# State-space heads of a two-block model: one full-height product spreads a head's step rows, two heads' half-width products alternate, and the scheduler's matmul costs are changed

## The chip, the cores and the metric

The kernel runs on one core of a Trainium2 chip. The metric is the device time of one execution in microseconds (us). Engines are named as the profile names them: PE is the matrix engine (TensorE), PEld its weight loads, DVE the vector engine, ACT the scalar engine, POOL the general engine (GpSimd), SP the engine that issues the transfers.

## What is computed

The program is a model of two blocks for 512 tokens of width 1024. Block 1 is a hybrid mixer, cross attention over a memory and a gated feed-forward part; block 2 has a layer with a long convolution (layer A) and a layer with sparse attention (layer B). The change is in the mixer's state-space part (SSD), 16 heads of 64 columns in two groups of 8, tokens in 4 chunks of 128:

```python
adt = (dt * a)...                       # a step per token and head
a_cs = jnp.cumsum(adt, axis=-1)         # cumulated within a chunk
seg = jnp.exp(where(causal, a_cs[l] - a_cs[s], -inf))
cb = einsum("bclgn,bcsgn->bgcls", cc, bc)
y_diag = einsum("bghcls,bcsghp->bclghp", cb * seg, xc)
y_off = einsum("bclgn,cbghpn,bghcl->bclghp", cc, prev, exp(a_cs))
y = y_diag + y_off                      # then + d_skip * xs, times silu(z)
```

`prev` holds the states at the starts of the chunks.

## The kernel before

All activations lie with the channels on the partitions and the 512 tokens along the row. Dense products run in three float32r products each (`mm3`): the weight and the activation are both split into a high and a low part (`whi`/`wlo`, and pairs of `act` tiles). Weights come by SP in tiles `raw`; ACT copies the high part `whi`, DVE subtracts to get the low part `wlo`. The dense results go to the PSUM banks `mm` (3 of them); the SSD part uses the banks `A` (2), `B` (2) and `C` (1).

Instructions are not issued in program order. Class `Program` records them all (each matmul, copy and transfer with an estimated duration `o.dur` and its dependencies, `rec`), then orders each engine's queue by a list schedule (`order`): priorities come from a pass over the reversed program (`latest`) blended with the last forward pass, 12 times over, and the best of the orders by its own estimate is emitted (`emit`). So every engine's queue is one fixed list, worked off strictly in that order, and the estimates decide where everything stands. All instructions are emitted at one line, which is why the profile calls nearly all of them L378.

The SSD part for one head:
- `head_a(hh)`: PE spreads the head's row of cumulated steps over all 128 partitions into a bank `A`. The weight is one column of `sel`, repeated; the moving operand is `arow`, rows of heads, split in a high and a low tile of 16 partitions, so that there are two products. DVE subtracts the head's column `acs` (a constant whose name in the profile is `dt`), takes min with 0, ACT the exponential, DVE multiplies by `cb`. The result is the tile `m`. ACT and POOL make `ce`, the decayed C rows, from the same bank.
- `head_b(hh)`: seven products, four with `m` and three with `ce`, each with a weight of 128 x 64 and a moving operand of 128 x 128 in float32, go to one half (64 partitions) of a bank `B`. Two heads share a bank. After the second, DVE adds the skip term from the bank and multiplies by `z`.
- `states(g, c)`: four transposes to a bank `C`, two DVE products from it, one product of 128 x 512 in float32 into a bank `B`, and the running state.

A loop over 18 steps calls `head_a(hh)`, and `head_b` two heads behind. Around it stand, in the program, the pool branch (`v_tile`, `p_tile`, and `om_pool`, whose 8 tiles of the output projection do not need the heads), and behind it the keys and values of the memory (`k_proj`, `v_proj`) and the output projection of the SSD branch.

In layer A, `conv_tile(j)` makes one of 12 channel tiles: one product with a diagonal matrix from `pad` into a bank `B`, then 19 multiply-adds by DVE on that bank (`B<-pad,vec,B` in the profile), the taps.

Of the kernel before, what the change touches and what calls it, by code (L numbers as in the profile page):

```python
# [17 lines left out]
P = 128  # L18
T = 512
# [39 lines left out]
class View:  # L59
    """a lazily resolved access pattern of a tile"""  # L60
# [61 lines left out]
class Program:  # L122
    """records instructions in program order, then orders each engine's by a list schedule"""
# [13 lines left out]
    def rec(s, eng, fn, m, args, kw):  # L137
# [27 lines left out]
        if eng == "PE":  # L165
            one = m == "transpose" or args[1].base.dt == F32R
            o.table = n > 8
            o.dur = n / 2.4 * 2 if m == "transpose" else max(107, n / 2.4) + 2.5 if one else max(27, n / 2.4) * 4
# [27 lines left out]
    def latest(s, prio):  # L196
        """latest starts, from a list schedule of the reversed program"""
# [35 lines left out]
    def order(s, prio, window):  # L233
# [9 lines left out]
        # slots in use if the rest ran in program order: a tile may take one early only if this never exceeds the number there is  # L243
# [137 lines left out]
def body(ctx, tc, t, out):  # L381
# [25 lines left out]
    def bank(tag):  # L407
        return new(pp, (P, T), F32, tag, True)
# [114 lines left out]
    class LN:  # L523
        """layer norm over tiles that come one by one, centred first by the mean of the first npil tiles, whose sum is then 0"""
# [29 lines left out]
        def finish(s):  # L554
            """broadcast rows r, q with norm = centred * r - q"""
# [36 lines left out]
    # ================= block 1, mixer =================  # L592
# [27 lines left out]
    # time steps of all heads  # L620
# [30 lines left out]
    # softplus(x) = max(x, 0) + log1p(exp(-|x|)), log1p(e) = 2 atanh(e / (2 + e))  # L651
# [20 lines left out]
    # cumulated steps as rows of heads  # L672
    ps = bank("B")[0:16, :]
    for c in range(4):
        TE.matmul(ps[:, c * P:(c + 1) * P], adt[:, c * 16:(c + 1) * 16], triu, start=True, stop=True)
    arow = split(ps)
    sel = const("sel", (16, 16), F32R)
    S.activation(sel, ident[0:16, 0:16], AF.Copy)
# [10 lines left out]
    # causal convolution of xs, B, C; order of the channel tiles: B0 B1 C0 C1, then xs  # L689
# [15 lines left out]
    # z gate  # L705
# [7 lines left out]
    # B in token rows, B C products  # L713
# [48 lines left out]
    def head_a(hh):  # L762
        g = hh // 8
        row = bank("A")
        for k in range(2):
            TE.matmul(row, sel[:, hh:hh + 1].to_broadcast([16, P]), arow[k], start=k == 0, stop=k == 1)
# [10 lines left out]
    ybank = [None]  # L777

    def head_b(hh):
        g, k = hh // 8, hh % 8  # L780
        m, ce = hd.pop(hh)
        if k % 2 == 0:
            ybank[0] = bank("B")
        yps = ybank[0]
        o = yps[64 * (k % 2):64 * (k % 2) + 64, :]
        for c in range(4):
            TE.matmul(o[:, c * P:(c + 1) * P], xdt[g][c][:, k * 64:(k + 1) * 64], m[:, c * P:(c + 1) * P],
                      start=True, stop=c == 0, skip_group_check=True)
            if c > 0:
                TE.matmul(o[:, c * P:(c + 1) * P], prev[g][c - 1][:, k * 64:(k + 1) * 64], ce[:, (c - 1) * P:c * P],  # L790
                          start=False, stop=True, skip_group_check=True)
        if k % 2 == 1:
            j = hh // 2
            y = conv[j]
            V.scalar_tensor_tensor(y, y, vc("d_skip", j), yps, op0=ALU.mult, op1=ALU.add)
            V.tensor_tensor(y, y, zs[j], op=ALU.mult)
            ysq.add(square(y))

    # multi-scale pool
# [49 lines left out]
    for hh in range(18):  # L849
        if hh < 16:  # L850
            head_a(hh)
        if hh >= 2:
            head_b(hh - 2)
        if 2 <= hh < 6:
            states(1, hh - 2)
    prog.shift -= SSD

    # keys and values of the first memory
# [675 lines left out]
```

## Time and profile before

| what | value |
|---|---|
| timed runs | 1705.38, 1706.32, 1707.93 us; median 1706.32 |
| profiled execution, first to last instruction (span) | 1705.8 us |
| PE busy | 1665.2 us, 98% of the span |
| PEld busy | 1361.4 us, 80% |
| DVE busy | 1142.2 us, 67% |
| ACT busy | 775.9 us, 45% |
| POOL busy | 421.0 us, 25% |
| DMA | 156.32 MB, mean 92 GB/s |

No separate time of the profiled execution is shown beside its span; the span lies inside the range of the timed runs, so what stands around it is within half a microsecond. Shares are averages over stages: PE is busy nearly everywhere, DVE between about half and almost all of the time depending on the stage. A busy PE is not a PE at its peak: matmuls overlap, and the spacing of their starts says more than the length of one. In the profile a product in float32 appears as two records, one in float32r as one.

### The profile page before, as it was taken

Reading aid. Unit: us, or ns where it says so; the run is one execution under the profiler, and the core shown is the slowest. Engines: PE = TensorE matmul, PEld = TensorE weight load, DVE = VectorE, ACT = ScalarE, POOL = GpSimd, SP = SyncE. Lnnn points to the kernel's source line nnn. Section 1 sums busy time; section 2 is a strip of 40 time slices with the busy share of each in tenths; the row PEclk is TensorE's granted clock in tenths of the full one; section 3 lists DMA queues with packets and bytes.
Section 4 is the critical chain, followed back from the end, with each engine's and each line's share of the span. In section 5 each row is a group of like instructions: output and inputs, shape, how many; then the busy total and the mean of one; then the engine's idle time right before and its main releaser. Section 6 shows DMA issues by size and latency. Waiting matters only on the chain. (4 is left out here: it accounts for less than half of the span.)

```text
span 1705.8 us, 21241 instructions
## 1 busy us (share of the span) xinstructions
PE 1665.2 (98%) x7966; PEld 1361.4 (80%) x7966; DVE 1142.2 (67%) x1801; ACT 775.9 (45%) x1349; POOL 421.0 (25%) x325
## 2 busy tenths in 40 slices
PE   9999999999999999999999997999899999999998
PEld 7888678888888888888878775778787788788886
DVE  7836778574565435544477999988747895467754
ACT  6722444444553222332356766545435434545541
POOL 1004433020031001201233678965630000000000
PEclk9999999999999999999999998999999999999999
DMA  7321212531242333322323311232233123211121
GB/s 242 117 86 56 93 50 87 160 99 50 75 131 93 98 99 99 95 79 90 117 91 108 102 56 50 81 127 87 75 124 115 62 99 94 80 63 50 53 84 50
DMA packets 49719, 156.32 MB, mean 92 GB/s; under 512 B 5648, under 2 KB 7568, under 8 KB 49616
## 3 DMA queue, kind: packets, MB, share of 16 engines
q1 hardware_dynamic: 49616, 154.96, 28.2%
q8 instruction: 63, 1.03, 0.3%
q14 instruction: 40, 0.33, 0.1%
HBM read 152.71 MB, written 2.10 MB: 91 GB/s over the span
## 5 line engine op out<-in xcount | busy, mean ns | idle before, releaser
L378 PE MATMUL mm<-act,whi 128*128 128x512 f32 (+1 forms) x3888 | 1194.3, 388 | 18.5 <-DVE act L378 12.9
L378 PEld LDWEIGHTS mm<-act,whi 128*128 128x128 f32 x3888 | 717.8, 189 | 174.3 <-ACT act L378 15.3
L378 PE MATMUL mm<-act,wlo 128*128 128x512 f32 (+1 forms) x1944 | 749.4, 388 | 9.8 <-DVE wlo L378 9.6
L378 ACT ACTIVATE whi<-raw 128x1024 fp32r<-128x1024 f32 (+3 forms) x293 | 289.4, 991 | 582.0 <-PE mm L378 352.5
L378 POOL TENSOR_TENSOR act<-act,act 128x512 f32<-128x512 f32 (+1 forms) x252 | 372.5, 1493 | 683.7 <-DVE act L378 314.8
L378 DVE TENSOR_TENSOR wlo<-raw,whi 128x1024 fp32r<-128x1024 f32 (+3 forms) x293 | 373.2, 1281 | 123.7 <-ACT whi L378 118.9
L378 PEld LDWEIGHTS mm<-act,wlo 128*128 128x128 f32 x1944 | 366.9, 189 | 85.5 <-DVE wlo L378 11.3
L378 DVE TENSOR_TENSOR act<-mm,act 128x512 f32<-128x512 f32 (+3 forms) x173 | 114.6, 664 | 244.9 <-PE mm L378 236.9
L378 ACT ACTIVATE act<-act 128x512 f32<-128x512 f32 (+2 forms) x222 | 134.7, 617 | 104.6 <-DVE act L378 65.9
L378 DVE SCALAR_TENSOR_TENSOR B<-pad,vec,B 128x512 f32<-128x512 f32 x228 | 167.2, 753 | 5.7 <-PE B L378 1.5
L378 DVE TENSOR_TENSOR act<-act,act 128x512 f32<-128x512 f32 (+3 forms) x203 | 138.3, 711 | 26.2 <-ACT act L378 25.3
L378 POOL TENSOR_TENSOR fr<-fv,mhalf 128x1 f32<-128x1 f32 x4 | 2.2, 547 | 410.5 <-DVE fv L378 410.5
L378 ACT ACTIVATE act<-pad,vec 128x512 f32<-128x512 f32 x144 | 94.8, 730 | 11.6 <-DVE pad L378 11.4
L378 PE MATMUL A<-act,act 128*128 128x256 f32 (+6 forms) x488 | 97.8, 342 | 0.3
L378 PEld LDWEIGHTS A<-act,act 128*128 128x128 f32 (+1 forms) x488 | 72.1, 189 | 16.7 <-issue 5.6
L378 PE MATMUL mm<-whi,act 128*128 128x512 f32 x264 | 85.0, 393 | 0.0
L378 ACT ACTIVATE act<-C 128x128 f32<-128x128 f32 (+4 forms) x164 | 52.2, 359 | 70.6 <-PE C L378 68.3
L378 PE MATMUL B<-act,act 128*128 128x128 f32 (+2 forms) x492 | 71.0, 284 | 0.0
L378 PEld LDWEIGHTS B<-act,act 128*128 128x128 f32 (+1 forms) x492 | 61.7, 167 | 9.6 <-issue 3.4
L378 ACT ACTIVATE act<-mm 128x512 f32<-128x512 f32 (+3 forms) x92 | 51.7, 566 | 18.4 <-PE mm L378 18.3
L378 PEld LDWEIGHTS mm<-whi,act 128*128 128x128 f32 x264 | 49.4, 188 | 9.6
L378 PE MATMUL mm<-wlo,act 128*128 128x512 f32 x132 | 51.8, 393 | 0.0
(130 smaller groups left out, 965.6 us busy)
## 6 DMA issues: line engine op xcount, KB each, us to landing
raw<-in_w_g_dram SPq DMA_DIRECT2D x22, 512.0 KB, 3.3
raw<-in_w_u_dram SPq DMA_DIRECT2D x22, 512.0 KB, 3.3
raw<-in_w_om_dram SPq DMA_DIRECT2D x16, 512.0 KB, 3.8
raw<-in_w_d_dram SPq DMA_DIRECT2D x16, 512.0 KB, 3.5
raw<-in_a_gate_dram SPq DMA_DIRECT2D x16, 512.0 KB, 3.4
raw<-in_b_gate_dram SPq DMA_DIRECT2D x16, 512.0 KB, 3.3
raw<-in_b_wo_dram SPq DMA_DIRECT2D x16, 512.0 KB, 3.3
raw<-in_w_xbc_dram SPq DMA_DIRECT2D x12, 512.0 KB, 4.2
```

What stands on the lines that cost most here:

```text
L378: r = o.fn(*[real(a) for a in o.args], **{k: real(v) for k, v in o.kw.items()})
```

## The change

Three parts. First, `arow` becomes one tile of 128 partitions: zero except rows 0 to 15 (high part) and 32 to 47 (low part), and `sel` has the unit columns at both places, so one product of 128 rows does what two of 16 rows did. To get both copies, the steps are laid out twice in `adt2` with 48 columns per chunk. Second, `head_b` takes a pair of heads, and the products of the two heads alternate (one into partitions 0 to 63, the next into 64 to 127). Third, the scheduler's estimate for matmuls is another formula. Comments and docstrings also go.

```diff
-            o.dur = n / 2.4 * 2 if m == "transpose" else max(107, n / 2.4) + 2.5 if one else max(27, n / 2.4) * 4
+            o.dur = 108.0 if m == "transpose" else max(112.0, n / 2.4 + 14) if one else 2 * max(111.0, n / 1.2 + 2)
...
-    ps = bank("B")[0:16, :]
+    arow = act(dt=F32R)
+    V.memset(f(arow), 0.0)
+    sel = const("sel", (P, 16), F32R)
+    S.activation(sel, ident[:, 0:16], AF.Copy, scale=0.0)
+    for o in (0, 32):
+        S.activation(sel[o:o + 16, :], ident[o:o + 16, o:o + 16], AF.Copy)
+    adt2 = const("adt2", (P, 4 * 48))
+    a2 = adt2.rearrange("p (c k) -> p c k", c=4)
+    V.memset(adt2, 0.0)
+    for o in (0, 32):
+        V.tensor_copy(a2[:, :, o:o + 16], v3(adt))
+    ps = bank("B")[0:48, :]
     for c in range(4):
-        TE.matmul(ps[:, c * P:(c + 1) * P], adt[:, c * 16:(c + 1) * 16], triu, start=True, stop=True)
-    arow = split(ps)
-    sel = const("sel", (16, 16), F32R)
-    S.activation(sel, ident[0:16, 0:16], AF.Copy)
+        TE.matmul(ps[:, c * P:(c + 1) * P], adt2[:, c * 48:(c + 1) * 48], triu, start=True, stop=True)
+    ahi = act(dt=F32R)[32:48, :]
+    S.activation(arow[0:16, :], ps[0:16, :], AF.Copy)
+    S.activation(ahi, ps[32:48, :], AF.Copy)
+    V.tensor_tensor(arow[32:48, :], ps[32:48, :], f(ahi), op=ALU.subtract)
...
-        for k in range(2):
-            TE.matmul(row, sel[:, hh:hh + 1].to_broadcast([16, P]), arow[k], start=k == 0, stop=k == 1)
+        TE.matmul(row, sel[:, hh:hh + 1].to_broadcast([P, P]), arow, start=True, stop=True)
...
-    def head_b(hh):
-        g, k = hh // 8, hh % 8
-        m, ce = hd.pop(hh)
-        if k % 2 == 0:
-            ybank[0] = bank("B")
-        yps = ybank[0]
-        o = yps[64 * (k % 2):64 * (k % 2) + 64, :]
+    def head_b(j):
+
+        g = j // 4
+        yps = bank("B")
+        pair = [(64 * i, (2 * j + i) % 8, *hd.pop(2 * j + i)) for i in range(2)]
         for c in range(4):
-            TE.matmul(o[:, c * P:(c + 1) * P], xdt[g][c][:, k * 64:(k + 1) * 64], m[:, c * P:(c + 1) * P],
-                      start=True, stop=c == 0, skip_group_check=True)
+            cc = slice(c * P, (c + 1) * P)
+            for o, k, m, ce in pair:
+                TE.matmul(yps[o:o + 64, cc], xdt[g][c][:, k * 64:(k + 1) * 64], m[:, cc], start=True, stop=c == 0, skip_group_check=True)
...
-        if hh >= 2:
-            head_b(hh - 2)
+        if hh >= 3 and hh % 2 == 1:
+            head_b((hh - 3) // 2)
```

What this does to the queues is seen at three places. The first is PE, in the second half of the SSD part. Before, with the output projection's products (`mm`) around it: seven products of one head (`act432` and `act433` are its tiles `m` and `ce`; the other operand is the weight), then two of the next head (`act436`), all into bank `B439`.

```order
L378 MATMUL mm325_2167<-act280_1672,wlo324_1907 128x512
L378 MATMUL B439_2262<-act432_2169,act370_1893 64x128
L378 MATMUL B439_2262<-act432_2169,act379_1952 64x128
L378 MATMUL B439_2262<-act433_2172,act373_1858 64x128
L378 MATMUL B439_2262<-act432_2169,act388_2015 64x128
L378 MATMUL B439_2262<-act433_2172,act382_1866 64x128
L378 MATMUL B439_2262<-act432_2169,act398_2033 64x128
L378 MATMUL B439_2262<-act433_2172,act391_1957 64x128
L378 MATMUL B439_2262<-act436_2208,act370_1893 64x128
L378 MATMUL B439_2262<-act436_2208,act379_1952 64x128
L378 MATMUL mm325_2167<-act286_1771,whi323_1841 128x512
```

The changed kernel, PE, two spread products (`sel`) and the pair that follows them: the heads of `act384` and `act392` take turns.

```order
L378 MATMUL A410_2113<-act46_119,sel_86 128x512
L378 MATMUL A415_2115<-act46_119,sel_86 128x512
L378 MATMUL B405_2120<-act384_1650,act343_1569 64x128
L378 MATMUL B405_2120<-act392_2031,act343_1569 64x128
L378 MATMUL B405_2120<-act384_1650,act348_1603 64x128
L378 MATMUL B405_2120<-act392_2031,act348_1603 64x128
L378 MATMUL B405_2120<-act385_1640,act346_1577 64x128
L378 MATMUL B405_2120<-act393_1826,act346_1577 64x128
L378 MATMUL B405_2120<-act384_1650,act353_1644 64x128
L378 MATMUL B405_2120<-act392_2031,act353_1644 64x128
```

Each spread is one product instead of two, and the half-width products of two heads stand in alternation. On PE as a whole the 112 half-width products stand in 16 separate runs before and in 12 after.

The second place is DVE, where the additions of `om_pool` (`mm305` to `mm333` are its eight result banks) meet the heads (`dt3` is `acs`; rows with a bank `A` are the heads' subtractions). Before, from the addition of the first of the eight tiles:

```order
L378 TENSOR_TENSOR act294_133<-mm305_1669,act294_133 128x512
L378 TENSOR_TENSOR act384_1843<-A383_1649,dt3_79 128x512
L378 TENSOR_TENSOR wlo320_1848<-raw318_1725,whi319_1833 128x1024
L378 TENSOR_SCALAR act384_1843<-act384_1843 128x512
L378 TENSOR_TENSOR act393_1861<-A392_1712,dt3_79 128x512
L378 SCALAR_TENSOR_TENSOR act79_509<-act79_509,vec_72,B368_1623 128x512
L378 TENSOR_TENSOR act295_135<-mm309_1701,act295_135 128x512
L378 TENSOR_TENSOR act384_1843<-act384_1843,act337_1374 128x512
```

The changed kernel, up to the addition of the seventh tile and what follows it:

```order
L378 TENSOR_TENSOR act298_145<-mm321_1927,act298_145 128x512
L378 TENSOR_TENSOR wlo465_1966<-raw463_1883,whi464_1957 128x1024
L378 TENSOR_TENSOR act299_147<-mm325_1959,act299_147 128x512
L378 TENSOR_TENSOR wlo472_1998<-raw470_1910,whi471_1989 128x1024
L378 TENSOR_TENSOR act300_149<-mm329_1991,act300_149 128x512
L378 TENSOR_TENSOR act392_2031<-A391_1665,dt3_79 128x512
L378 TENSOR_TENSOR act379_2038<-C378_1782,dt6_82 128x512
L378 TENSOR_TENSOR act356_2028<-B355_1642,act356_2028 128x512
L378 TENSOR_TENSOR act400_2053<-A399_1715,dt3_79 128x512
L378 TENSOR_SCALAR act392_2031<-act392_2031 128x512
```

Before, the heads' vector work was spread among the eight additions; now eleven of the sixteen heads stand behind the seventh. On PE, likewise, 157 products of `om_pool` stand in one piece, and nine of the sixteen spreads and 100 of the 112 half-width products behind them.

The third place is DVE in layer A, around the weight split `wlo1640`. Before (the taps of two channel tiles in `B1571` and `B1609`, then the split):

```order
L378 SCALAR_TENSOR_TENSOR B1571_8261<-pad1559_7775,vec2_73,B1571_8261 128x512
L378 SCALAR_TENSOR_TENSOR B1609_8371<-pad1597_7986,vec2_73,B1609_8371 128x512
L378 TENSOR_TENSOR wlo1640_8439<-raw1638_8153,whi1639_8233 128x1024
L378 TENSOR_TENSOR wlo1644_8441<-raw1642_8248,whi1643_8313 128x1024
L378 TENSOR_TENSOR wlo1582_8447<-raw1580_8110,whi1581_8341 128x512
```

The changed kernel:

```order
L378 TENSOR_TENSOR act1560_8203<-act1560_8203,B1571_8206 128x512
L378 SCALAR_TENSOR_TENSOR B1609_8323<-pad1597_7967,vec2_73,B1609_8323 128x512
L378 SCALAR_TENSOR_TENSOR act1501_8432<-A1500_8305,act1392_7715 128x512
L378 SCALAR_TENSOR_TENSOR B1609_8323<-pad1597_7967,vec2_73,B1609_8323 128x512
L378 SCALAR_TENSOR_TENSOR act1573_8440<-A1572_8418,act1398_7990 128x512
L378 SCALAR_TENSOR_TENSOR B1609_8323<-pad1597_7967,vec2_73,B1609_8323 128x512 x2
L378 TENSOR_TENSOR wlo1640_8448<-raw1638_8108,whi1639_8171 128x1024
```

The split has moved back: counted from the split `wlo1515`, which stands ahead of it in both, it is the 99th DVE instruction before and the 106th now (77 and 83 of them taps), while on PE 195 dense products stand between the first use of `wlo1515` and that of `wlo1640` before and 186 now. The last of the twelve products with `pad` stands 44 rows of PE's queue earlier than before. Apart from shifts of this kind, layer A, the feed-forward part and layer B stand nearly as they did on every engine.

## Rows read from the trace of the kernel before

**Rows 1.** The page: the span, the busy time of PE (us, share of the span, instructions), and the granted TensorE clock in 40 equal slices of the span, in tenths of full speed (9 is 90% or more).
```profile
span 1705.8 us, 21241 instructions
PE 1665.2 (98%) x7966; PEld 1361.4 (80%) x7966; DVE 1142.2 (67%) x1801; ACT 775.9 (45%) x1349; POOL 421.0 (25%) x325
PEclk9999999999999999999999998999999999999999
```

**Rows 2.** The waits of PE, longest first in total: who waited for whom, us in total, times, longest.
```profile
PE mm L378 <- DVE act L378: 12.9, 11, 5.9
PE mm L378 <- DVE wlo L378: 9.6, 2, 9.2
PE mm L378 <- ACT act L378: 4.3, 4, 1.5
```

**Rows 3.** Groups of PE's instructions by tile and shape (weights' rows*columns, then the moving operand): records, busy us, mean ns of one. The half-width products of the heads, and the spread products.
```profile
L378 PE MATMUL B<-act,act 128*64 128x128 f32 x224 | 26.1, 277 | 0.0
L378 PE MATMUL A<-act,sel 16*128 16x512 f32 x32 | 11.6, 441 | 0.0
```

**Rows 4.** PE in order of time: start in us, length, records merged. One state product (float32, two records) and two dense products up to the next row; then two spread pairs among dense products; then a plain stretch of dense products (30 from the first start to the second).
```profile
223.46 1.02 PE L378 MATMUL B<-act,act 128*128 128x512 f32 x2
...
224.77 0.39 PE L378 MATMUL mm<-act,wlo 128*128 128x512 f32 x1
...
236.48 0.39 PE L378 MATMUL mm<-act,wlo 128*128 128x512 f32 x1
236.79 0.73 PE L378 MATMUL A<-act,sel 16*128 16x512 f32 x2
237.45 0.50 PE L378 MATMUL mm<-act,whi 128*128 128x512 f32 x1
237.88 0.72 PE L378 MATMUL A<-act,sel 16*128 16x512 f32 x2
238.53 0.50 PE L378 MATMUL mm<-act,whi 128*128 128x512 f32 x1
238.87 0.39 PE L378 MATMUL mm<-act,wlo 128*128 128x512 f32 x1
...
275.02 0.39 PE L378 MATMUL mm<-act,wlo 128*128 128x512 f32 x1
...
281.82 0.39 PE L378 MATMUL mm<-act,wlo 128*128 128x512 f32 x1
```

**Rows 5.** PE in order of time at three runs of half-width products: one head alone, two heads one after the other, and the place of the first listing above.
```profile
241.71 1.74 PE L378 MATMUL B<-act,act 128*64 128x128 f32 x14
243.38 0.50 PE L378 MATMUL mm<-act,wlo 128*128 128x512 f32 x1
...
251.68 2.89 PE L378 MATMUL B<-act,act 128*64 128x128 f32 x28
254.50 0.50 PE L378 MATMUL mm<-act,wlo 128*128 128x512 f32 x1
...
266.15 0.40 PE L378 MATMUL mm<-act,wlo 128*128 128x512 f32 x1
266.48 1.80 PE L378 MATMUL B<-act,act 128*64 128x128 f32 x18
268.21 0.73 PE L378 MATMUL mm<-act,whi 128*128 128x512 f32 x2
268.78 0.39 PE L378 MATMUL mm<-act,wlo 128*128 128x512 f32 x1
```

**Rows 6.** The first and last start of the products that make the cumulated step rows (ns min/median/max of one, first and last start), and PE's first spread product.
```profile
L378 PE MATMUL B<-triu,dt x8: 272/273/282, 49.2 to 49.9; 128*16 128x128 f32 x8
162.56 0.49 PE L378 MATMUL A<-act,sel 16*128 16x512 f32 x1
```

**Rows 7.** Groups of DVE's instructions by tile and shape: busy us, mean ns of one, idle us before them. In this order: taps of layer A, a head's multiplication (and others of that form), a head's subtraction, a head's minimum, the products from a transposed bank, the skip term of a pair, the split of a weight tile.
```profile
L378 DVE SCALAR_TENSOR_TENSOR B<-pad,vec,B 128x512 f32<-128x512 f32 x228 | 167.2, 753 | 5.7 <-PE B L378 1.5
L378 DVE TENSOR_TENSOR act<-act,act 128x512 f32<-128x512 f32 x97 | 66.0, 720 | 7.1 <-ACT act L378 6.6
L378 DVE TENSOR_TENSOR act<-A,dt 128x512 f32<-128x512 f32 x16 | 10.9, 686 | 5.9 <-PE B L378 2.8 <-ACT act L378 1.6 <-PE A L378 1.4
L378 DVE TENSOR_SCALAR act<-act 128x512 f32<-128x512 f32 x17 | 7.8, 487 | 0.0
L378 DVE TENSOR_TENSOR act<-C,dt 128x512 f32<-128x512 f32 x14 | 9.5, 685 | 2.0 <-PE mm L378 1.3 <-PE C L378 0.6
L378 DVE SCALAR_TENSOR_TENSOR act<-act,vec,B 128x512 f32<-128x512 f32 x8 | 5.9, 736 | 0.0
L378 DVE TENSOR_TENSOR wlo<-raw,whi 128x1024 fp32r<-128x1024 f32 x245 | 331.6, 1359 | 112.8 <-ACT whi L378 111.2 <-ACT act L378 0.8
```

**Rows 8.** Busy time of the engines in two stretches (us from the span's start): one in the SSD part, one in layer A; behind the five engines the granted clock.
```profile
230.00:260.00 30.00, 30.00 (x166) 21.71 (x165) 22.99 (x36) 12.19 (x21) 10.10 (x10) 1.00 0.11 36
1020.00:1060.00 40.00, 30.64 (x118) 22.59 (x117) 39.11 (x59) 23.14 (x41) 36.56 (x28) 0.87 0.18 55
```

**Rows 9.** PE in order of time at two of its waits (in brackets the idle us before the row, and what ended it), and DVE at the second of them.
```profile
203.01 0.73 PE L378 MATMUL mm<-act,whi 128*128 128x512 f32 x2 [1.50 <-ACT act L378]
...
1047.68 0.79 PE L378 MATMUL mm<-act,wlo 128*128 128x512 f32 x1 [9.23 <-DVE wlo L378]
...
1034.54 11.96 DVE L378 SCALAR_TENSOR_TENSOR B<-pad,vec,B 128x512 f32<-128x512 f32 x18
1046.41 2.96 DVE L378 TENSOR_TENSOR wlo<-raw,whi 128x1024 fp32r<-128x1024 f32 x3
```

More of the change, by code (lines that the diff above doesn't have):

```diff
@@ L775, in head_a @@
         hd[hh] = (m, ce)
-    ybank = [None]
-    def head_b(hh):
-        g, k = hh // 8, hh % 8
-        m, ce = hd.pop(hh)
-        if k % 2 == 0:
-            ybank[0] = bank("B")
-        yps = ybank[0]
-        o = yps[64 * (k % 2):64 * (k % 2) + 64, :]
+    def head_b(j):
+        g = j // 4
+        yps = bank("B")
+        pair = [(64 * i, (2 * j + i) % 8, *hd.pop(2 * j + i)) for i in range(2)]
         for c in range(4):
-            TE.matmul(o[:, c * P:(c + 1) * P], xdt[g][c][:, k * 64:(k + 1) * 64], m[:, c * P:(c + 1) * P],
-                      start=True, stop=c == 0, skip_group_check=True)
+            cc = slice(c * P, (c + 1) * P)
+            for o, k, m, ce in pair:
+                TE.matmul(yps[o:o + 64, cc], xdt[g][c][:, k * 64:(k + 1) * 64], m[:, cc], start=True, stop=c == 0, skip_group_check=True)
             if c > 0:
[L790 to L797, printed above, removed]
+                for o, k, m, ce in pair:
+                    TE.matmul(yps[o:o + 64, cc], prev[g][c - 1][:, k * 64:(k + 1) * 64], ce[:, (c - 1) * P:c * P],
+                              start=False, stop=True, skip_group_check=True)
+        y = conv[j]
+        V.scalar_tensor_tensor(y, y, vc("d_skip", j), yps, op0=ALU.mult, op1=ALU.add)
+        V.tensor_tensor(y, y, zs[j], op=ALU.mult)
+        ysq.add(square(y))
     icnt = const("icnt", (P, 64))
```

## The prediction

> **What bounds the kernel now.** I read the page first, then PE's waits, then PE in order of time where the heads stand, then DVE's groups there and in layer A. The page says that PE is busy for 1665.2 of 1705.8 us [rows 1]. PE's waits that have a releaser are few: the three largest groups come to 26.8 us, most of it for DVE [rows 2]. So PE's queue sets the time nearly everywhere, and work taken from it counts in full unless a wait takes its place. What a product costs there is the spacing of starts: 30 dense products take 281.82 - 275.02 = 6.80 us, 0.227 each [rows 4]. The sum is made against the span, which is within half a microsecond of the median; I start from 1706.3.
>
> **The spread products.** Two spread pairs among dense products [rows 4]: from 237.45 to 238.87 there are two dense products and one pair, 1.42 us. Less 2 x 0.227, the pair costs 0.97, far more than two dense products: each spread starts 0.33 after the last, and the dense products around it are late by about a tenth each. A product of 128 rows on the same bank has the form of a dense one and should cost 0.227. That gives 16 x (0.97 - 0.23) = 11.8 us as the most. The least is the busy time of the 32 spreads, 11.6 [rows 3], less 16 x 0.227 = 3.6: 8.0. Some pairs stand next to each other or next to half-width products and share their edges, so I take **-10.4**.
>
> **The half-width products.** One head alone is seven products, 14 records, and takes 243.38 - 241.71 = 1.67 us [rows 5], 0.12 a record. Around such a run the neighbours lose time: 266.48 - 266.15 is 0.33 instead of 0.227 ahead, and the two dense products behind take 268.78 - 268.21 = 0.57 instead of 0.45, so 0.21 a run. Now: 26.1 us [rows 3] + 16 runs x 0.21 = 29.5.
>
> Whether alternation helps is decided by what two heads cost when they meet. The run at 266.48 has seven products of one head and two of the next, 18 records, and takes 268.21 - 266.48 = 1.73 us; the 14 of one head take 1.67. Four records of the other half cost 0.06 us instead of 4 x 0.12 = 0.48. The run of 28 records takes 254.50 - 251.68 = 2.82 instead of 2 x 1.67 = 3.34 [rows 5]. So the end of one head's stream and the beginning of the other's go side by side, each at its own pace; today only the few records that the queue holds at the seam do. In alternation the two streams are always at hand, and a pair should take about what one head takes. Then eight pairs cost 8 x 1.67 = 13.4 us, 12 runs x 0.21 = 2.5, and I add 1.4 for runs that are cut within a pair (an estimate: eight products stand without a partner there, half of 0.24 each, and four more runs than pairs at a record each): 17.3. That is 29.5 - 17.3 = **-12.2**. If nothing overlaps, 16 heads cost 16 x 1.67 = 26.7 and 12 runs 2.5, 29.2 in all, and the change gives 0.3; these are the two bounds, and I take the first because the seam shows it.
>
> A rule of the Trainium skill speaks against this. The page "TensorE: Matmul & The Clock Gate", section "Part 3: Packing small matmuls — row/col tiling", says that a weight load overlaps running matmuls only when its row group differs, and that matmuls start and end strictly in order. The two heads here share all 128 rows and differ in columns only, so by its letter each load would wait. The trace disagrees at the seam (1.73 against 1.67). By the rule the sum below would end near 1703.
>
> **What is added.** The setup (two clears, two small copies, three copies of `sel`, one more on ACT) lies on DVE and ACT before the cumulated rows, which are made at 49.2 us, while the first spread runs at 162.56 [rows 6]: 113 us of cover, cost 0. Without it each instruction would cost well under a microsecond. The four products for the rows have wider weights and the same moving operand: 0. No transfer is added.
>
> **What moves: the heads.** Eleven heads' vector work now stands behind the seventh addition of `om_pool`, where DVE had before worked on heads between the additions and was busy for 22.99 of 30 us with PE at 30.00 [rows 8]. In that stretch, up to the last pair, DVE has eleven subtractions, minima and multiplications, 11 x (0.686 + 0.487 + 0.720) = 20.8, seven products from banks `C` and `B` at 0.685 = 4.8, five skip terms at 0.736 = 3.7, and one weight split, 1.4: 30.7 us [rows 7]. PE has in the same stretch 24 dense products, 5.4; nine spreads, 2.0; 86 half-width products, six pairs at 1.67 and a bit, 10.8, and ten runs x 0.21, 2.1; three state products, each 1.31 - 0.45 = 0.86 [rows 4], 2.6; and eight transposes, fifteen products of half length and four sums, about 3.4 at a tenth each. That is 26.3 (5.4 + 2.0 + 12.9 + 2.6 + 3.4). Both start together, since the seventh tile's last product releases DVE. So PE waits here for about 4 us where it waited for nothing; those behind are the next spreads, as only two banks `A` exist and DVE empties them. The bounds are 0 (means count a little overlap between instructions) and 9 (each chain through ACT seen in full). I take **+4**. The wait at 203.01, 1.50 [rows 9], stands at the same step of `om_pool` in both orders, and I leave it.
>
> **What moves: layer A.** The longest wait, 9.23 us at 1047.68, is for the split `wlo1640`: DVE is in 18 taps from 1034.54 to 1046.41, 0.66 each, and only then reaches it [rows 9]; DVE is busy 39.11 of 40 us there, with the clock at 0.87 of full, part of the time at the lower of its two levels, 1.2 GHz [rows 8]. The new order puts seven more DVE instructions ahead of that split, 7 x 0.66 = 4.6, and nine dense products fewer on PE, 2.0, with four short ones more: the wait grows by about 6, to 15. DVE's total in this layer is the same, and the last product with `pad` comes earlier; what DVE did early here it need not do later, where PE waits for it too, 5.9 at the longest [rows 2]. About half comes back: **+3**, with -9 (the wait goes) and +8 as bounds.
>
> **The sum.** 1706.3 - 10.4 - 12.2 + 4 + 3 = 1690.7; I predict **1691 us**.
>
> **The rivals.**
> - *The waits don't grow, or shrink* (the new estimates fit PE's real spacing: 0.227 for a dense product is what the new formula says, 0.216 the old one). For it: DVE has free time in the SSD part [rows 8]. Against it: in both places the counts above put more DVE work ahead of PE's need. 1706.3 - 22.6 = 1683.7 without new waits, 1674 if the 9.23 goes as well.
> - *The heads don't run side by side*, as by the skill's rule; the change then does only what the spreads give. 1706.3 - 10.4 - 0.3 + 7 = 1702.6. Against it: the seam at 266.48.
> - *The split in layer A turns the gain round.* The wait for `wlo1640` takes the place of the work removed. It could reach the whole run of DVE ahead of the split: 48 rows in the new order, mostly taps, some 31 us, if PE came to the first use just as that run begins. Then 1706.3 - 22.6 + 4 + (31 - 9.2) = 1709.5, slower. It decides from a wait of some 28 us on, 9.2 + 22.6 - 4. Against it: today DVE's run begins while PE still works on tiles that were split before it, and 186 dense products, 42 us, still stand between the two uses.
>
> **How the numbers follow.** Runs of this kernel lie within 0.15% of each other; 0.2%, 3.4 us, is about what can be told from no change. The forecast, PE's gain less some waits: 0.60, its own range 1685 to 1698. Waits not grown or less: 0.18, 1674 to 1685. No overlap: 0.10, of which half stays above 3.4 us of gain. Layer A turns it: 0.05, slower. More wait than the bounds of the forecast but no loss, 1698 to 1704: 0.07, a part of it within 0.2%. To leave out two in ten, the range cuts the lower end of the second case and the turn: 1680 to 1702. Faster 0.88, same 0.07, slower 0.05.
>
> **What would show it.** Right: 16 spread records at 128 rows with dense spacing; runs of 28 half-width records near 1.7 us; PE's busy time down by about 22 us; new waits of PE on banks `A` or on `m` near the end of the SSD part; a wait of 12 to 16 us at `wlo1640`. Wrong: runs of 28 at 3 us or more; a full-height spread slower than 0.227; PE's waits in the SSD part or in layer A more than 10 us above today's, or the clock at its lower level for long there because PE paused more often.

## The result and the profile after

The changed kernel takes 1724.27 us (1720.51 to 1726.77), the kernel before 1706.22 beside it: a ratio of 1.0101, interval 1.0087 to 1.0115. It is 1% slower, where 1691 was forecast.

The page of the changed kernel, to be read against [rows 1]:

```profile
span 1723.3 us, 21213 instructions
PE 1661.8 (96%) x7950; PEld 1359.2 (79%) x7950; DVE 1149.8 (67%) x1805; ACT 771.2 (45%) x1350; POOL 412.2 (24%) x325
PEclk9999998999999999999999998999899999999999
```

PE's busy time fell by 3.4 us only, and the span grew by 17.5: PE is idle for 61.5 us instead of 40.6. Its longest waits (who for whom, us, times, longest), against [rows 2]:

```profile
PE mm L378 <- DVE act L378: 17.7, 17, 7.8
PE mm L378 <- ACT act L378: 12.4, 9, 6.7
PE C L378 <- ACT act L378: 7.2, 4, 4.4
PE mm L378 <- DVE wlo L378: 6.1, 4, 2.9
PE B L378 <- DVE act L378: 4.0, 4, 1.8
```

The work that the change was about did shrink. The groups of [rows 3] (records, busy us, mean ns) are now these, 26.1 against 17.3 and 11.6 against 7.1 us, in spite of a part at half clock:

```profile
L378 PE MATMUL B<-act,act 128*64 128x128 f32 x224 | 17.3, 295 | 4.1 <-DVE act L378 4.0
L378 PE MATMUL A<-act,sel 128*128 128x512 f32 x16 | 7.1, 456 | 0.2
```

To see where it went, cut the program at three products that every kernel here has, PE's first sum over partitions (`C<-ones`) in three norms: the one behind the SSD part, the final one of block 1, and the one behind layer A. Four stretches: first (with the heads), middle, layer A, end. In each: its length, busy us of PE, PEld, DVE, ACT, POOL, then the granted clock. Before:

```profile
0.00:326.80 326.80, 321.88 (x1605) 256.98 (x1605) 227.91 (x346) 149.72 (x220) 76.69 (x79) 0.99 0.34 112
326.80:856.30 529.50, 528.69 (x2434) 440.66 (x2433) 270.35 (x332) 196.77 (x320) 75.12 (x57) 1.00 0.30 94
856.30:1284.80 428.50, 404.03 (x1839) 325.32 (x1838) 360.06 (x469) 239.21 (x402) 265.97 (x184) 0.98 0.28 90
1284.80:1705.80 421.00, 410.65 (x2096) 338.48 (x2094) 283.87 (x655) 190.17 (x411) 3.21 (x5) 0.99 0.23 75
```

After:

```profile
0.00:331.10 331.10, 309.29 (x1590) 250.33 (x1590) 227.16 (x351) 146.34 (x221) 80.09 (x79) 0.97 0.33 110
331.10:860.20 529.10, 528.49 (x2429) 439.63 (x2427) 274.10 (x332) 195.98 (x318) 74.83 (x57) 1.00 0.29 94
860.20:1300.50 440.30, 411.37 (x1841) 328.75 (x1841) 364.67 (x469) 238.94 (x402) 254.08 (x184) 0.97 0.27 88
1300.50:1723.30 422.80, 412.67 (x2097) 340.47 (x2095) 283.89 (x655) 189.96 (x411) 3.20 (x5) 0.99 0.22 74
```

The first stretch is 4.3 us longer, not 18 shorter; layer A is 11.8 longer; the end 1.8; the middle is the same.

One more step makes the stretches comparable. From a stretch's length take PE's idle time (*idle*), and half of the time in which PE was busy at the lower of its two clock levels, 1.2 GHz, as the trace's clock records give it (*clock*, what that level cost). What is left is PE's work at full clock, called *work* below. In us:

| kernel | time | first: length | idle | clock | work | layer A: length | idle | clock | work |
|---|---|---|---|---|---|---|---|---|---|
| before | 1706.2 | 326.8 | 4.9 | 1.7 | 320.2 | 428.5 | 24.5 | 3.9 | 400.2 |
| after | 1724.3 | 331.1 | 21.8 | 7.6 | 301.7 | 440.3 | 28.9 | 9.3 | 402.0 |
| sched | 1722.1 | 330.1 | 9.0 | 3.3 | 317.8 | 440.3 | 28.9 | 9.3 | 402.1 |
| heads | 1716.6 | 316.5 | 15.3 | 2.8 | 298.4 | 447.0 | 31.9 | 15.6 | 399.5 |
| spread | 1719.6 | 320.9 | 9.9 | 3.0 | 308.0 | 447.4 | 34.3 | 13.6 | 399.6 |
| pair | 1727.4 | 329.6 | 16.8 | 3.1 | 309.7 | 447.3 | 30.3 | 17.9 | 399.1 |
| heads_p7 | 1698.8 | 318.3 | 15.8 | 3.2 | 299.2 | 427.0 | 22.7 | 4.0 | 400.3 |
| before_p8 | 1729.0 | 331.5 | 5.5 | 5.1 | 320.9 | 444.5 | 31.8 | 13.3 | 399.4 |
| spread_p7 | 1710.8 | 330.4 | 16.0 | 6.0 | 308.4 | 427.1 | 22.6 | 4.3 | 400.2 |
| pair_p7 | 1721.0 | 343.3 | 20.1 | 13.5 | 309.8 | 427.2 | 22.5 | 4.4 | 400.3 |
| before_p10 | 1723.1 | 328.0 | 5.7 | 1.7 | 320.6 | 443.0 | 33.5 | 8.5 | 401.0 |
| sched_p7 | 1733.0 | 332.2 | 11.4 | 6.4 | 314.4 | 447.7 | 34.5 | 11.5 | 401.7 |
| heads_seq | 1697.8 | 319.1 | 10.3 | 3.4 | 305.4 | 427.2 | 22.7 | 4.3 | 400.2 |
| heads_known | 1709.7 | 327.0 | 18.9 | 7.7 | 300.4 | 428.8 | 23.5 | 5.4 | 399.9 |
| after_known | 1727.8 | 333.3 | 25.9 | 10.5 | 296.9 | 441.1 | 27.8 | 11.2 | 402.1 |
| after_thin | 1717.6 | 326.0 | 17.7 | 6.7 | 301.6 | 439.9 | 27.4 | 10.7 | 401.8 |
| heads_pool | 1695.3 | 315.8 | 12.7 | 3.3 | 299.8 | 427.2 | 22.8 | 4.1 | 400.2 |
| heads_late30 | 1712.6 | 331.7 | 6.0 | 1.7 | 324.0 | 429.1 | 23.3 | 5.8 | 400.0 |
| heads_late40 | 1714.2 | 333.8 | 6.3 | 1.6 | 325.9 | 428.4 | 23.7 | 4.4 | 400.3 |

The middle is 529.1 to 529.8 in all of these, the end 420.9 to 423.0. The kernels below the second are the experiments. The work of layer A is the same in all of them to within 3 us, though its length differs by 21: what differs there is waits and clock. One of them, `after_late`, has no line, since its profiled execution took 9 us more than its others.

### The profile page after: what moved, and what is told of

It is laid out like the page before. It is cut to its first block, busy times and chain, and to the rows that moved or that the text cites. A ratio compares the mean times of both kernels' runs of the same rounds, so it can differ in the third digit from the quotient of the medians.

```text
span 1723.3 us, 21213 instructions
## 1 busy us (share of the span) xinstructions
PE 1661.8 (96%) x7950; PEld 1359.2 (79%) x7950; DVE 1149.8 (67%) x1805; ACT 771.2 (45%) x1350; POOL 412.2 (24%) x325
## 3 DMA queue, kind: packets, MB, share of 16 engines
q1 hardware_dynamic: 49616, 154.96, 27.4%
## 5 line engine op out<-in xcount | busy, mean ns | idle before, releaser
L378 PE MATMUL mm<-act,whi 128*128 128x512 f32 (+1 forms) x3888 | 1202.4, 390 | 31.4 <-DVE act L378 17.7
L378 PEld LDWEIGHTS mm<-act,whi 128*128 128x128 f32 x3888 | 723.8, 190 | 187.2 <-DVE act L378 17.7
L378 POOL TENSOR_TENSOR act<-act,act 128x512 f32<-128x512 f32 (+1 forms) x252 | 363.7, 1455 | 648.8 <-DVE act L378 317.2
L378 DVE TENSOR_TENSOR act<-act,act 128x512 f32<-128x512 f32 (+4 forms) x203 | 146.0, 751 | 18.7 <-ACT act L378 17.8
L378 PE MATMUL B<-act,act 128*128 128x128 f32 (+2 forms) x492 | 60.6, 292 | 4.1 <-DVE act L378 4.0
L378 PEld LDWEIGHTS B<-act,act 128*128 128x128 f32 (+1 forms) x492 | 51.3, 171 | 13.0 <-DVE act L378 4.7
L378 PE MATMUL C<-ident,act 128*128 128x128 f32 (+1 forms) x288 | 50.0, 279 | 8.1 <-ACT act L378 7.2
```

What stands on the lines that cost most here:

```text
L378: r = o.fn(*[real(a) for a in o.args], **{k: real(v) for k, v in o.kw.items()})
```

## The experiments

**One part at a time.** `sched` is the kernel before with the new line for `o.dur` alone; `heads` the changed kernel with the old line; `spread` and `pair` the one or the other edit on the kernel before, with the old line. `heads` against the changed kernel:

```diff
-            o.dur = 108.0 if m == "transpose" else max(112.0, n / 2.4 + 14) if one else 2 * max(111.0, n / 1.2 + 2)
+            o.dur = n / 2.4 * 2 if m == "transpose" else max(107, n / 2.4) + 2.5 if one else max(27, n / 2.4) * 4
```

> The kernel before with the new matmul estimates alone; the state-space part is untouched. Theory A (the two edits of the heads give about 22 us on PE, and the new estimates' queue loses about 40 in waits and at the lower clock): 1735 to 1750 us. Theory B (the heads in their new form make the waits, the estimates are harmless): 1700 to 1710. Theory C (each redrawn queue lands by luck within some 10 us of its neighbours, whatever the edit): anywhere from 1700 to 1725, and not the sum of the parts.

> Both edits of the heads with the old matmul estimates. Theory A: 1706 - 22 = 1684, with 1680 to 1692. Theory B: 1718 to 1728, as the full change. Theory C: 1684 give or take 10.

> The full-height spread alone, old estimates, heads one after the other. Theory A: 1706 - 10 = 1696. Theory B: 1706 to 1716, if the spread's new setup or earlier heads wait. Theory C: 1696 give or take 10.

> The alternating pairs alone, old estimates, two 16-row spreads per head. Theory A: 1706 - 12 = 1694. Theory B: 1710 to 1720, since a pair waits for both heads. If alternation saves nothing on PE: 1706. Theory C: 1694 give or take 10.

Measured: 1722.11, 1716.58, 1719.58 and 1727.40 us; all four are slower than before (ratios 1.0077, 1.0053, 1.0067, 1.0115). The losses of the parts don't add up to that of the whole, and the new estimates alone, with no edit of the heads, lose nearly as much as the full change. A and B fall as they were put; C holds for `sched`, but its 10 us are too few for `heads`, `spread` and `pair`. The table says why. The work in the first stretch falls about as forecast: by 12.2 us for `spread`, 10.5 for `pair`, 21.8 for `heads`. But layer A, which holds not one changed instruction, takes 447 us in the three kernels with old estimates and 440 in the two with new ones, against 428.5. This is its row in `sched`, to be set beside the one of the changed kernel above:

```profile
859.40:1299.70 440.30, 411.38 (x1842) 328.83 (x1840) 363.75 (x469) 238.87 (x402) 254.40 (x184) 0.97 0.27 88
```

In the two traces PE, DVE, ACT and POOL work off layer A in the same order, so the changed kernel's loss there comes with the order that the new estimates led to, and not with the heads.

**The planner's pass.** The planner orders the program 13 times and emits the order that its own estimate likes best; each pass is a whole new order. Compared instruction by instruction, PE's and DVE's queues of layer A are, in `heads`, `spread` and `pair`, those of the eighth pass, while the kernel before emits the seventh; and the seventh passes of `heads` and of the kernel before are identical there. The planner had put the eighth of `heads` ahead by 3 us, and the eighth of the kernel before behind by 0.7. So four kernels with the pass set by hand (`it` counts from 0; `before_p8` has 7 in place of 6):

```diff
-            if r[1] < best[1]:
+            if it == 6:
                 best, prio = r, w
```

> Both edits of the heads, old estimates, and the planner is made to emit its seventh pass, the one that the kernel before emits, and not the eighth, which it had chosen by 3 us of its own estimate. From the cross attention's end on the queues of PE and DVE are then those of the kernel before. Theory D (layer A's queue costs 18 us, whatever stands in the state-space part): 1716.6 - 18 = 1698, with 1694 to 1702. Theory B (the heads in their new form lose it by waits): 1710 or more.

> The kernel before without any edit of its work or its estimates; it emits the planner's eighth pass instead of the seventh (by its own estimate 0.7 us longer). Theory D: 1706 + 18 = 1724, with the stretch of layer A at 352 us where the kernel before takes 333. If the queue of the eighth pass is harmless and the edits lost the time: 1704 to 1710.

> The full-height spread alone, with the seventh pass. Theory D: 1719.6 - 18.9 = 1701, that is 5 us faster than before, half of the 10.4 forecast. Otherwise 1715 or more.

> The alternating pairs alone, with the seventh pass. Theory D: 1727.4 - 18.6 = 1709, slower than before by 3, so that the waits of the pairs in the state-space part outweigh what PE saves. If the pairs are free of loss when the order is that of before: 1694.

Measured: `heads_p7` 1698.77, ratio 0.9945 (0.9928 to 0.9961), faster than both kernels; `before_p8` 1729.04, ratio 1.0124 (1.0108 to 1.0139), with no edit at all. Layer A follows the pass: 427.0 to 427.2 us in the edited kernels with the seventh and 428.5 in the kernel before, 447.0 to 447.4 with the eighth and 444.5 in `before_p8`. (That run ends 5 us above the 1724 expected, since its first stretch is 4.7 us longer too.) In `heads_p7` the old wait for the weight's low part is back to the hundredth [rows 9]:

```profile
1039.25 0.79 PE L378 MATMUL mm<-act,wlo 128*128 128x512 f32 x1 [9.23 <-DVE wlo L378]
```

And in `before_p8` layer A is this row, 16 us longer than before: 7.3 more of waits, 9.4 more for the clock, 0.8 less work:

```profile
861.00:1305.50 444.50, 412.73 (x1838) 331.99 (x1837) 363.36 (x469) 238.68 (x402) 250.68 (x184) 0.96 0.26 87
```

Theory D stands for layer A. `spread_p7` (1710.75 for 1701) and `pair_p7` (1720.99 for 1709) miss by 10 and 12, and not in layer A: their first stretch is 10 and 14 us longer than in the eighth pass, nearly all of it waits and clock. The first stretch is redrawn as well.

**Is it the estimates or the draw?** `before_p10` is the kernel before with its tenth pass, `sched_p7` is `sched` with its seventh.

> The kernel before, no edit of its work or estimates, the planner's tenth pass (its own estimate is 2.3 us above the seventh). Theory E (each pass has its own layer A on the chip, by luck, and the planner's estimates can't tell them apart): layer A between 427 and 447 us, not 428.5, and the whole between 1706 and 1730. Theory F (old estimates give a good layer A, and only the new ones or the eighth pass spoil it): layer A 428 to 431.

> The kernel before with the new matmul estimates, seventh pass instead of the third. Theory E: layer A away from the third pass's 440 by several us in either direction. Theory F: 440 give or take 2, and the end part 423 as in the third, since the new estimates make it.

Measured: 1723.14 with layer A 443.0, and 1733.03 with 447.7. Theory F falls on both: old estimates give 428, 443 and 445, new ones 440 and 448. Of the passes tried here the one in the kernel before is by far the best, and nothing in the planner's estimates (within 2.3 us of each other for the three old ones) tells it from the rest. In layer A the new estimates' two passes are no worse than the old ones' other two.

**Does the alternation overlap, and who pays?** `heads_seq` is `heads_p7` with the same queues, except that where products of both heads of a pair stand next to each other, the first head's come first.

```diff
+                move[pe[j - 1].idx] = sorted(pe[i:j], key=lambda o: o.half[1])
```

> Both edits of the heads, seventh pass, all queues as there, but wherever products of both heads of a pair stand next to each other, those of the first head come first and then those of the second. If alternation is what saves PE's time: 10 to 12 us more busy time on PE, 1704 to 1711 in all. If nothing overlaps or the seam gives it anyway: 1699.

Measured: 1697.82, the same as `heads_p7`. PE in order of time at one run of two pairs, `heads_p7` and then `heads_seq`:

```profile
252.61 3.33 PE L378 MATMUL B<-act,act 128*64 128x128 f32 x56
```

```profile
253.83 5.19 PE L389 MATMUL B<-act,act 128*64 128x128 f32 x56
```

So alternation does run two heads side by side, 3.33 against 5.19 us. In the table the work rises by 6.2 us, and idle time and clock fall by 5.3: what alternation saves PE in `heads_p7`, PE spends waiting. The expectation priced the work too high, at 10 to 12, and the end wrong; that the end comes near the 1699 of its other case isn't for that case's reason, since the products do overlap. In `heads_p7` the end of this stretch isn't set by PE.

**What PE waits for behind the heads.** The wait stands at a product for the memory's keys, 7.76 us at 293.76 in the changed kernel: three banks `mm` are full, and DVE empties them only after its splits. `after_thin` takes DVE work away in the changed kernel's queues, `heads_pool` POOL work in those of `heads_p7`. `o.thin` is set for DVE's products of `m` with `cb` and of `y` with `z` in the one, for POOL's sums of the squares of `y` in the other.

```diff
+            cut = (lambda a: a[:, 0:64]) if o.thin else (lambda a: a)
+            r = o.fn(*[cut(real(a)) for a in o.args], **{k: real(v) for k, v in o.kw.items()})
```

> The changed kernel with its queues as they are, but DVE's multiplication of m by the chunk products and its gating of y by z work on 64 of 512 columns, so that part of the result is left out: DVE has 24 x 0.53 = 12.7 us less to do in the state-space part, PE the same work. If DVE's speed behind om_pool sets when PE gets on (the wait of 7.76 before the memory's keys and those on the banks B): the first stretch shrinks by 8 to 14 us, the whole to 1710 to 1717. If the waits come from ACT, the transfers or from where single instructions stand: 1721 to 1725.

> Both edits of the heads, old estimates, seventh pass, all queues as there, but six of POOL's additions of the squares of y work on 64 of 512 columns, so that the norm is wrong by what is left out. If DVE's splits of y beside them take 1.1 to 1.8 us instead of 0.74 because POOL works at the same time: DVE gains some 5 us there, the wait of 6.6 before the keys shrinks to 1 to 3, and the whole is 1690 to 1695. If they are slow for another reason: 1697 to 1701.

Measured: `after_thin` 1717.64, 6.6 less, with the first stretch 5.1 us shorter: below the 8 to 14 expected, and the whole just above the 1710 to 1717. Of 12.7 us taken from DVE less than half arrives, and the wait before the keys is still 7.1, because PE comes earlier too. `heads_pool`: 1695.26, the wait 3.17 instead of 6.60, both a little above what was expected. DVE at the same place (two splits of y with a scale), and PE's wait, in `heads_p7`:

```profile
272.55 3.49 DVE L378 SCALAR_TENSOR_TENSOR act<-act,vec,act 128x512 fp32r<-128x512 f32 x2
287.77 0.77 PE L378 MATMUL mm<-act,whi 128*128 128x256 f32 x2 [6.60 <-DVE act L378]
```

and in `heads_pool`:

```profile
272.45 1.54 DVE L379 SCALAR_TENSOR_TENSOR act<-act,vec,act 128x512 fp32r<-128x512 f32 x2
285.37 0.48 PE L379 MATMUL mm<-act,whi 128*128 128x256 f32 x2 [3.17 <-DVE act L379]
```

Two splits take 1.54 us when POOL isn't adding 512 columns beside them, 3.49 when it is. DVE's lateness is part of the cause, and POOL part of DVE's.

**Does the planner misplace PE?** It prices a half-width product at 213 or 222 ns, twice what it costs in alternation. `heads_known` and `after_known` halve that.

```diff
+            if not one and int(args[0].shape[0]) == 64:
+                o.dur = 111.0
```

> Both edits of the heads, old estimates, seventh pass, and the planner's price of a half-width product is halved to 111 ns, about what it costs in alternation; the queues from the cross attention on stay those of the seventh pass. Theory G (the planner thinks PE some 12 us later at the memory's keys than it is, and puts the weight normalisation's splits ahead of the additions that empty the banks): the wait of 6.6 before the keys falls to under 2, the first stretch from 318 to 306 to 311, the whole 1686 to 1692. Theory H (DVE has too much to do behind the heads in any order): the first stretch stays at 316 to 320, the whole 1697 to 1701. Theory C (draws): anything between 308 and 330 in the first stretch.

> The changed kernel with its new estimates and the same halved price for the half-width products; the planner again picks its third pass, and from the cross attention on the queues are those of the changed kernel. Theory G: the first stretch from 331 to 315 to 320, the whole 1708 to 1713. Theory H: 1721 to 1726. Theory C: anything between 315 and 335 in the first stretch.

Measured: 1709.71 and 1727.75 (first stretch 327.0 and 333.3, waits before the keys 6.1 and 5.9). Both are slower than with the wrong price. Theory G falls. H gave 316 to 320, so H as it was put falls too; only "a new draw" fits.

**The projection moved.** From 220 to 240 us DVE parts the kernels: in the traces so far it is busy for 15 us or more where spreads stand between the products of `om_pool`, for 6 to 10 where seven or more of the sixteen heads' spreads stand behind them. DVE's busy time from 220 to 240 and from 240 to 280 (then clock, DMA share, GB/s), before and after:

```profile
220.00:240.00 20.00, 15.01 (x22) 1.00 0.17 54
240.00:280.00 40.00, 35.98 (x49) 1.00 0.13 40
```

```profile
220.00:240.00 20.00, 7.67 (x8) 1.00 0.36 120
240.00:280.00 40.00, 36.99 (x60) 0.96 0.12 40
```

So the three last kernels put `om_pool` off by a constant in the pass that they emit. `heads_late30` is shown; `heads_late40` has `j >= 2` and 40000, `after_late` all `j`, 60000 and the third pass.

```diff
+            if it == 6:
+                w = [p - o.early for p, o in zip(w, s.ops)]
...
+            if o.eng in ("PE", "DVE") and j >= 4:
+                o.early = -30000.0
```

> Both edits of the heads, old estimates, seventh pass, and in that pass om_pool's fifth to eighth tile are put off by 30 us of priority: the last seven spreads stand behind 825 to 849 dense products of the first stretch instead of 902 to 912, about where they stand before the change (768 to 841). Queues from the cross attention on as in heads_p7. Theory I (the heads behind the block leave DVE idle from 220 to 240 and overload it behind): DVE 12 us or more in 220 to 240, no wait over 3 before the memory's keys, the first stretch from 318 to 306 to 312, the whole 1686 to 1693. Theory H (DVE is overloaded in any order): 1697 to 1701.

> The same with om_pool's third to eighth tile put off by 40 us: the last eight spreads stand behind 768 to 802 dense products, earlier than before the change. Theory I: the first stretch 304 to 311, the whole 1684 to 1692. Theory H: 1697 to 1701.

> The changed kernel with its new estimates and its third pass, all eight tiles of om_pool put off by 60 us: the last nine spreads stand behind 767 to 803 dense products instead of 896 to 904; queues from the cross attention on as in the changed kernel. Theory I: the first stretch from 331 to 308 to 316, the whole 1701 to 1710, the rest of the loss being layer A. Theory H: 1720 to 1725.

Measured: 1712.55, 1714.21 and 1720.68. The times of the first two lie above both theories. The first half of theory I holds: in `heads_late30` DVE is busy for 14.51 of these 20 us, PE's idle time falls from 15.8 to 6.0 and what the clock cost from 3.2 to 1.7, as low as before the change, and no wait is left before the keys. But the work rises from 299.2 to 324.0. PE in order of time in `heads_late30`:

```profile
247.22 0.43 PE L380 MATMUL B<-act,act 128*64 128x128 f32 x2
247.58 0.49 PE L380 MATMUL mm<-act,whi 128*128 128x512 f32 x1
248.00 0.43 PE L380 MATMUL B<-act,act 128*64 128x128 f32 x2
248.37 0.49 PE L380 MATMUL mm<-act,whi 128*128 128x512 f32 x1
```

The planner put the half-width products one by one between dense ones, 65 runs instead of 13. One half-width and one dense product take 0.79 us (248.37 - 247.58 and the like); less 0.227 for the dense one that is 0.56, where alternation costs 3.33 / 28 = 0.12 a product. In `after_late` the runs stay long (55 products in one) and the work at 301, and DVE is busy for 18.21 us from 220 to 240; but PE's waits in the first stretch of its trace come to 19.1 us still, most of them now at 202 to 218 and 258 to 272 us. Theory I's 1701 to 1710 is missed, and H's 1720 to 1725 is met.

Not tried: two 16-row spreads in place of the one, in an otherwise fixed queue.

## Why the prediction was wrong, by its steps

- **The spread products, -10.4**: right. The work of `spread` and `spread_p7` is 12.2 and 11.8 below before. Between dense products of the changed kernel a spread has their spacing, 244.82 - 244.60 (0.23 to 0.24 at seven of the sixteen; at the others, most of them beside half-width products, 0.32 and more):

```profile
244.60 0.39 PE L378 MATMUL A<-act,sel 128*128 128x512 f32 x1
244.82 0.39 PE L378 MATMUL mm<-act,wlo 128*128 128x512 f32 x1
253.08 1.75 PE L378 MATMUL B<-act,act 128*64 128x128 f32 x28
265.14 1.75 PE L378 MATMUL B<-act,act 128*64 128x128 f32 x28 [1.32 <-DVE act L378]
275.19 3.13 PE L378 MATMUL B<-act,act 128*64 128x128 f32 x28 [1.83 <-DVE act L378]
293.76 0.77 PE L378 MATMUL mm<-act,whi 128*128 128x256 f32 x2 [7.76 <-DVE act L378]
```

- **The half-width products, -12.2**: right. A run of 28 records takes 1.75 us, where one head's 14 took 1.74 before [rows 5]; the work is 10.5 and 10.4 less in `pair` and `pair_p7`. Both edits together: 21.8 in `heads`, 21.0 in `heads_p7`, 22.6 forecast. In the changed kernel it is 18.5, and 16.1 against `sched`, which has the same estimates: redrawing the order moves the work by some microseconds as well (2.4 in `sched`, 5.8 in `sched_p7`, without an edit of the heads). The seam of [rows 5] was the right evidence, and the rule that spoke against it doesn't hold for these two column halves.
- **The setup, 0**: nothing speaks against it; PE's waits ahead of the first spread come to 2.7 us before and 3.5 in `heads`, all of them in the first 27 us.
- **New waits in the SSD part, +4 (0 to 9)**: this step failed. Idle time and clock in the first stretch went from 6.6 to 29.4, +22.8. The sum compared DVE's and PE's loads from `om_pool`'s seventh tile to the last pair and stopped there. The longest wait is behind it, 7.76 us for the banks of the memory's keys, because DVE does the weights' splits and eight splits of y first, several of them at more than twice their time beside POOL:

```profile
277.42 3.46 DVE L378 SCALAR_TENSOR_TENSOR act<-act,vec,act 128x512 fp32r<-128x512 f32 x2
282.66 1.79 DVE L378 SCALAR_TENSOR_TENSOR act<-act,vec,act 128x512 fp32r<-128x512 f32 x1
276.10 11.72 POOL L378 TENSOR_TENSOR act<-act,act 128x512 f32<-128x512 f32 x6
```

  It priced no clock either: PE runs at the lower level (1.2 GHz) in these rows, while and after it waits (length, PE busy, clock):

```profile
207.00:213.00 6.00, 5.29 (x12) 0.51 0.28 87
276.00:278.00 2.00, 2.00 (x22) 0.50 0.48 186
290.00:299.00 9.00, 5.24 (x24) 0.50 0.33 117
```

  The clock is 5.9 of the 22.8; the pair at 275.19 takes 3.13 instead of 1.75 in it. And it counted work saved on PE as time saved in a stretch that PE no longer sets: in the order of `heads_p7`, `heads_seq` gives 6 us of it back at no cost. PE's waits more than 10 us above before (+16.9 here) were among the prediction's own signs of being wrong.
- **"The wait at 203.01 stands at the same step in both orders, and I leave it"**: right for that wait, which is 1.53 at 207.58 now, at the product with as many dense ones ahead of it (766) as before. But a second one has come up just ahead, 1.59 at 204.58, and the stretch at half clock behind them is 6.8 us long instead of 3.4.
- **Layer A, +3 (-9 to +8)**: this step failed too, in kind. Measured +11.8: 4.4 of waits, 5.4 for the clock, 1.8 of work. The named wait for `wlo1640` did not grow from 9.23 to 15; it shrank to 2.41. Yet its product comes 8.0 us later, counted from the stretch's start (1059.59 - 860.2 against 1047.68 - 856.3), because others stand ahead, and PE is at the lower clock from 1046.8 to 1053.6:

```profile
1045.88 0.66 PE L378 MATMUL C<-ident,act 128*128 128x128 f32 x4 [4.36 <-ACT act L378]
1048.09 1.11 PE L378 MATMUL C<-ident,act 128*128 128x128 f32 x4 [1.55 <-ACT act L378]
1059.59 0.50 PE L378 MATMUL mm<-act,wlo 128*128 128x512 f32 x1 [2.41 <-DVE wlo L378]
1104.31 0.50 PE L378 MATMUL mm<-act,wlo 128*128 128x512 f32 x1 [2.94 <-DVE wlo L378]
```

  The text followed one wait through a queue that had been redrawn all along. `sched` has the same order and the same loss here without the heads' edits, and `before_p8` and `before_p10` show that such a draw costs 14 to 16 us here with no edit at all, which no bound of the sum held.
- **The rivals**: "layer A turns the gain round" had the right side and stretch, and the wrong mechanism. The sum should have had a term for the new draw as a whole: the four other orders of the unchanged work (`sched`, `sched_p7`, `before_p8`, `before_p10`) end 15 to 25 us above the kernel before.

What it comes to in the changed kernel: -18.5 of work and +22.8 of waits and clock in the first stretch, +11.8 in layer A, +1.8 in the end, -0.4 in the middle: 17.5, the difference of the spans. Against `sched`, the heads' two edits save 16.1 of work in the first stretch and cost 17.1 of waits and clock there.

Open: what makes the first stretch's waits and clock 7 us in one order and 36 in another. DVE's idle time beside `om_pool` and its load behind it go with it in most traces but not in `after_late`; DVE's lateness is a part, as `after_thin` and `heads_pool` show, and moving the heads removes the waits in `heads_late30`. No kernel here has long alternating runs and a DVE that keeps up, so whether both can be had isn't shown.

## What to carry to other kernels

When a planner fixes every queue, an edit anywhere can redraw the queues everywhere, and a tuned kernel may stand on a lucky draw, as this one did: time it against other draws of the same work (another pass, no edit) before an edit is credited or blamed. Cut the program at instructions that both kernels have, and take waits and lower clock apart from work in each stretch (counting time that PE idles at the lower clock once, as waiting); that showed in one table that the edits did what they should and where the gain went. Then fix the good queue: `heads_p7`, the two edits with the pass of the kernel before, takes 1698.8 us and beats both.

## What the runs showed of the hardware

Float32 products into the two halves of the output partitions run side by side when they alternate, with all 128 rows in use: 56 records in 3.33 us, 5.19 head after head. A single one between dense products costs 0.56 us, with what its neighbours lose. The Trainium skill's page "TensorEngine Tiling (Array Packing)", section "Tiling Modes", says that the tiles of a mode, such as its two of 128 x 64, work independently, and that a change of the tiling mode drains the engine. The traces agree with the first by 3.33 against 5.19; the 0.56 is in line with the second, but no run here tells a drain from other costs of the change.

A DVE split with two operands in SBUF takes 0.77 us when POOL adds 64 columns beside it and 1.75 when it adds 512 (1.54 and 3.49 for two). The Trainium skill's page "SBUF — State Buffer", section "Who interferes with whom", says that such an instruction and one of GpSimd that reads SBUF contend, and that the lock is exclusive; `heads_pool` agrees that they contend. DVE's instruction of the same kind with a bank as its last operand (`act<-act,vec,B`) is not slowed: 0.74 at 270.83 in `heads_p7`, with POOL adding 512 columns from 270.51 to 277.20.
